# Merge gates kept raw until the merge, and the convolution's SiLU as one ScalarE function, in a one-layer hybrid decoder

## Chip, cores and metric

The kernel runs on one core of one Trainium2 chip. The metric is the device time of one execution in microseconds (us). All arithmetic is in float32; the large matrix products are made of three passes of a rounded float32 type (fp32r).

## What is computed

One layer takes 256 prompt tokens and 64 sample tokens (8 sequences of 8), so 320 columns in all, through a SwiGLU feed-forward, a token mixer and a second SwiGLU feed-forward. The change touches three places of the mixer: the SiLU behind the short convolution, and the two sigmoid gates of the merge. The reference, cut to them:

```
qk_pre, mv, mo, mif, aq, ak, av, gm, ga = split_cols(h @ w_in)
qk, conv_new = causal_conv(qk_pre, conv_buf, conv_w, conv_b)
qk = jax.nn.silu(qk).astype(f32)
mq = qk[..., :QK_WIDTH // 2].reshape(B, T, M_HEADS, M_DK)
mk = qk[..., QK_WIDTH // 2:].reshape(B, T, M_HEADS, M_DK) * (M_DK ** -0.5)
...
merged = jax.nn.sigmoid(gm) * (hm.astype(dt) @ w_pm) + jax.nn.sigmoid(ga) * (ha.reshape(B, T, A_WIDTH).astype(dt) @ w_pa)
return merged @ w_out, (k_new, v_new, C1, n1, m1, conv_new)
```

`hm` is the mLSTM's output, `ha` that of the dilated attention. M_DK is 256, so the factor on `mk` is 1/16.

## The kernel before

The program is a list of jobs that `run_job` (L272) walks in a fixed order. A job is a matrix product of 256 output rows: its weights come in chunks of 128x1024 values (512 KB, tile `raw`, five buffers). Each chunk is split by ScalarE into a rounded half `hi` (L225) and by VectorE into the remainder `lo` (L226), three buffers each, and TensorE then makes 24 matmuls of 320 columns from it into the PSUM tile `fg` (two buffers). A split is written into the program two chunks ahead of its matmuls. When a job's last chunk is done, its result is taken out of PSUM by an "evac" function during the next job.

Between the chunks, generators are stepped: the evac functions that yield (list `every`), the mLSTM recurrence (`mlstm`, L994, in `odd`, so every second chunk), the prompt attention (`even`) and the sample attention (`slow`, 8 steps in 15 chunks). What a generator issues at a step goes into the same in-order queue of its engine as the splits. So the order of all engines is set by these steps, and an instruction that waits holds up everything behind it on its engine. All DMAs but a few are issued from the SP queue (L141), also in order.

The mixer's jobs are: attention q, k, v (4 times, `aq_evac`, `ak_evac`, `av_evac`) and the input/forget gates; then four times mLSTM v, two convolved q/k jobs (`qk_evac`, L922) and the output gate (`mo_evac`, L988); then 16 merge-gate jobs; then 8 jobs with `w_pm` (`pm_evac`, L1377), 8 with `w_pa` (`pa_evac`, L1403) and 8 with `w_out`. The sample attention reads the key and value caches during most of this, and the mLSTM reads and writes its state matrices.

`qk_evac` makes SiLU as y/(1+exp(-y)): an Exp on ScalarE (L951), 1+ and for j >= 4 also x16 on GpSimd (L952), two reciprocals on VectorE with a yield before each (L955), a product on GpSimd (L956), then the store to `qk_d`. `sigmoid_evac` (L978) takes a gate out of PSUM on VectorE (L409), makes an Exp on ScalarE (L981), 1+ on GpSimd (L982), two reciprocals on VectorE (L985) and a store to DRAM; the four `mo` jobs and the 16 merge-gate jobs use it. The merge jobs load a gate back (`load_pair`) and multiply.

GpSimd also makes `qm` (L1037) and `ks` (L1048), the stationary operands of the mLSTM's small matmuls, and `qbd` (L702) for the sample attention. ScalarE changes its function table where Exp, Ln, Sqrt and SiLU follow each other; these ACT_TABLE_LOAD instructions are put in when the program is built.

Of the kernel before, what the change touches and what calls it, by code (L numbers as in the profile page):

```python
# [9 lines left out]
F32 = mybir.dt.float32  # L10
F32R = mybir.dt.float32r
AF = mybir.ActivationFunctionType
OP = mybir.AluOpType
# [17 lines left out]
C_MV, C_MO, C_MIF, C_AQ, C_AK, C_AV, C_GM, C_GA = 2048, 3072, 4096, 4104, 5128, 6152, 7176, 9224  # L31
# [97 lines left out]
def decoder_kernel(tc, I, O, K):  # L129
    nc = tc.nc  # L130
    V, S, G, T = nc.vector, nc.scalar, nc.gpsimd, nc.tensor
# [8 lines left out]
    def dma(out, in_):  # L140
        nc.sync.dma_start(out, in_)  # L141
# [4 lines left out]
    def bcast(ap, n, at=1):  # L146
        shape = list(ap.shape)
        shape.insert(at, n)
        idx = [slice(None)] * len(ap.shape)
        idx.insert(at, None)  # L150
        return ap[tuple(idx)].to_broadcast(shape)
# [6 lines left out]
    def later(fn, n=1):  # L158
        later_q.append([n, fn])
# [23 lines left out]
    def spawn(g, lst=None, first=False):  # L183
        lst = every if lst is None else lst
        lst.insert(0 if first else len(lst), g)
# [44 lines left out]
    def wsrc(w, k0, nk, c0):  # L230
        return w[k0 * 128:(k0 + nk) * 128, c0:c0 + 256].rearrange("(k p) c -> p k c", p=128)
# [3 lines left out]
    def add_job(w, k0, nkt, c0, mov, evac, kind="w", setup=None):  # L235
        cs = []
        if kind == "mif":
            cs.append((len(chunks), 0, 16))
            chunks.append((w[0:D, C_MIF:C_MIF + 8].rearrange("(k p) c -> p k c", p=128), 16, "mif"))
        else:  # L240
            k = 0
            while k < nkt:
                nk = min(4, nkt - k)
                cs.append((len(chunks), k, nk))
                chunks.append((wsrc(w, k0 + k, nk, c0), nk, "w"))
                k += nk
        jobs.append((cs, nkt, mov, evac, kind, setup))
# [95 lines left out]
    gate_d = dp.tile([16, 128, 2 * NT], F32, name="gate_d")  # L343
# [26 lines left out]
    def t_tile(dt=F32, name="tt"):  # L370
        return xp.tile([128, 2, NT], dt, tag="t", bufs=19, name=name)
# [36 lines left out]
    def times_rstd(out, ps):  # L408
        V.tensor_tensor(out, ps[:, :, 0:NT], bcast(rstd, 2), op=OP.mult)  # L409
# [96 lines left out]
    w_in = I["w_in"][0]  # L506
# [11 lines left out]
    def m3_full(name):  # L518
        return mxt([128, 3, 257], "m3", 3, name)
# [402 lines left out]
    def qk_evac(ps, j):  # L922
        pret = m3_full("pre").rearrange("p a b -> p (a b)")
        pre = pret[:, 0:694].rearrange("p (m c) -> p m c", m=2)
        V.tensor_tensor(pre[:, :, 3:259], ps[:, :, 0:SEQ], bcast(rstd[:, 0:SEQ], 2), op=OP.mult)
        pres = pre[:, :, 259:347].rearrange("p m (b c) -> p m b c", b=8)
        V.tensor_tensor(pres[:, :, :, 3:11], ps[:, :, SEQ:NT].rearrange("p m (b t) -> p m b t", b=8),
                        bcast(rstd[:, SEQ:NT].rearrange("p (b t) -> p b t", b=8), 2), op=OP.mult)
        G.memset(pre[:, :, 0:3], 0.0)
        G.tensor_copy(pres[:, :, :, 0:3], convst[:, 2 * j:2 * j + 2].rearrange("p m (b c) -> p m b c", b=8))  # L930
        cvn = M["cvn"]
        G.tensor_copy(cvn[:, 2 * j:2 * j + 2, 0:3], pre[:, :, 256:259])
        G.tensor_copy(cvn[:, 2 * j:2 * j + 2, 3:27].rearrange("p m (b c) -> p m b c", b=8), pres[:, :, :, 8:11])
        yield
        y = t_tile(F32, "y")
        for m in range(2):
            if m:
                yield
            kt = 2 * j + m
            for i in range(4):  # L940
                w = gv[:, G_CW + 16 * i + kt:G_CW + 16 * i + kt + 1]
                for o, x in ((y[:, m, 0:SEQ], pre[:, m, i:i + SEQ]),
                             (y[:, m, SEQ:NT].rearrange("p (b t) -> p b t", b=8), pres[:, m, :, i:i + 8])):
                    if i == 0:
                        S.activation(o, x, AF.Identity, scale=w, bias=gv[:, G_CB + kt:G_CB + kt + 1])
                    else:
                        V.scalar_tensor_tensor(o, x, w, o, op0=OP.mult, op1=OP.add)
        yield
        yv = y
        e = pret[:, 0:2 * NT].rearrange("p (m c) -> p m c", m=2)  # L950
        S.activation(e, yv, AF.Exp, scale=-1.0)  # L951
        G.tensor_scalar(e, e, 1.0, 1.0 if j < 4 else 16.0, op0=OP.add, op1=OP.mult)  # L952
        for m in range(2):
            yield
            V.reciprocal(e[:, m], e[:, m])  # L955
        G.tensor_tensor(e, yv, e, op=OP.mult)  # L956
        yield
        dma(qk_d[j].rearrange("p (a n) -> p a n", a=2), e)
        M["qk"] += 1
        if M["qk"] == 2:  # L960
            spawn(mlstm(), odd)
        if M["qk"] == 8:
            spawn(conv_out(), even)

    def conv_out():
        yield
        for q in range(4):
            ps = bg_tile()
            for k in range(4):
                c0 = 27 * (4 * q + k)  # L970
                tr(ps[:, k * 128:(k + 1) * 128], M["cvf"][:, c0:c0 + 128])
            cs = m3_full("cs").rearrange("p a b -> p (a b)")[:, 0:512]
            S.copy(cs[0:27], ps[0:27])
            later(lambda cs=cs, q=q: dma(O["conv_prompt"].rearrange("o b r c -> (o b r) c")[:, q * 512:(q + 1) * 512], cs[0:3]), 2)
            later(lambda cs=cs, q=q: dma(O["conv_sample"].rearrange("o b r c -> (o b r) c")[:, q * 512:(q + 1) * 512], cs[3:27]), 2)
            yield

    def sigmoid_evac(ps, dst):  # L978
        t = t_tile(F32, "sg")
        times_rstd(t, ps)  # L980
        S.activation(t, t, AF.Exp, scale=-1.0)  # L981
        G.tensor_scalar(t, t, 1.0, None, op0=OP.add)  # L982
        for m in range(2):
            yield
            V.reciprocal(t[:, m], t[:, m])  # L985
        later(lambda: dma(dst, t.rearrange("p a n -> p (a n)")), 2)

    def mo_evac(ps, h):  # L988
        yield from sigmoid_evac(ps, mo_d[h])
        yield  # L990
        yield
        M["mo"] = h
# [321 lines left out]
    for h in range(4):  # L1314
        add_job(w_in, 0, 16, C_MV + h * 256, mov_x, lambda ps, h=h: mv_evac(ps, h))
        for j in (h, h + 4):
            add_job(w_in, 0, 16, j * 256, mov_x, lambda ps, j=j: qk_evac(ps, j))
        add_job(w_in, 0, 16, C_MO + h * 256, mov_x, lambda ps, h=h: mo_evac(ps, h))
    for j in range(8):
        add_job(w_in, 0, 16, C_GM + j * 256, mov_x, lambda ps, j=j: sigmoid_evac(ps, gate_d[j]))  # L1320
    for j in range(8):
        add_job(w_in, 0, 16, C_GA + j * 256, mov_x, lambda ps, j=j: sigmoid_evac(ps, gate_d[8 + j]),
                setup=(lambda: spawn(presplit("hr"))) if j == 7 else None)


# [5 lines left out]
    def split_act(r, pool_tile):  # L1331
        hi, lo = pool_tile(F32R, "bh"), pool_tile(F32R, "bl")
        split(r, hi, lo)
        return hi, lo
# [3 lines left out]
    def presplit(key):  # L1338
        while key not in M:
            yield  # L1340
        for h in range(2):
            PRE[key, h] = split_act(M[key][h], t_tile)
            yield
# [33 lines left out]
    def pm_evac(ps, j):  # L1377
        sg = GT.pop(j)
        MT[j] = sg
        V.tensor_tensor(sg, ps[:, :, 0:NT], sg, op=OP.mult)  # L1380

    def pa_open():
# [19 lines left out]

    def pa_evac(ps, j):  # L1403
        sg = GT.pop(j)
        V.tensor_tensor(sg, ps[:, :, 0:NT], sg, op=OP.mult)
        V.tensor_tensor(sg, sg, MT[j], op=OP.add)
        H_H[j], H_L[j] = split_act(sg, h_tile)
# [8 lines left out]
    for j in range(8):  # L1416
        add_job(I["w_pm"][0], 0, 8, j * 256, mov_b, lambda ps, j=j: pm_evac(ps, j),
                setup=lambda j=j: pm_setup(j))
    for j in range(8):
        add_job(I["w_pa"][0], 0, 8, j * 256, mov_b, lambda ps, j=j: pa_evac(ps, j),  # L1420
                setup=lambda j=j: pa_setup(j))
# [48 lines left out]
    def last_tr(m):  # L1470
        xn, a = Y["xn"], bg_tile()
        for t, t0 in enumerate(TOK):
            tr(a[:, t * 128:(t + 1) * 128], xn[:, m, t0:t0 + 128])
        return a
# [204 lines left out]
    a = last_tr(1)  # L1679
# [56 lines left out]
```

## Time and profile before

| | |
|---|---|
| three timed runs | 2787.8, 2794.57, 2795.02 us (median 2794.57) |
| profiled execution, its own time | 2789.53 us |
| its span in the trace | 2787.7 us |
| busy in the span: TensorE, VectorE, ScalarE, GpSimd | 2730.3, 1633.2, 1082.7, 231.4 us |
| mean DMA rate | 200 GB/s |
| mixer with sample attention and mLSTM | about 980 to 1700 us of the span |

The span runs from the first to the last instruction. PE is TensorE's matmul row, DVE is VectorE, ACT ScalarE, POOL GpSimd and SP the queue that issues DMAs. A matmul is pipelined, so PE's busy time overstates its work; its waits and its granted clock are the better reading. "DMA share" is the mean busy share of the 16 DMA engines.

### The profile page before, as it was taken

What the parts mean: (1) busy time and instruction counts of PE and PEld (TensorE: products, weight loads), DVE (VectorE), ACT (ScalarE), POOL (GpSimd) and SP (SyncE); (2) the same over time, 40 slices, a digit from 0 to 9 for tenths busy, and PEclk for the clock granted to TensorE, in tenths of its full rate; (3) what the DMA queues carried; (4) which work ended last, traced back from release to release, by engine and by line L of the source; (5) the groups of instructions that cost most, each with busy time, mean ns of one, the idle gap of its engine ahead of it and who ended that gap; (6) DMA issues with size and microseconds to landing.
All of it is one profiled execution on the core that took longest, in us unless ns stands there. A gap on an engine that the chain in (4) does not pass through costs nothing.

```text
span 2787.7 us, 51237 instructions
## 1 busy us (share of the span) xinstructions
PE 2730.3 (98%) x21522; PEld 2678.7 (96%) x21522; DVE 1633.2 (59%) x1863; ACT 1082.7 (39%) x1364; POOL 231.4 (8%) x258
## 2 busy tenths in 40 slices
PE   9999999999999999989999999999999999999998
PEld 8999999999999999988889889999999999999998
DVE  6444444444446656977988886755444444444444
ACT  5333333333335333434443433444333333333344
POOL 0100000000000000122322210000000000000000
PEclk9999999999999999989999999999999999999999
DMA  6555555555556689999999988655554555545543
GB/s 216 160 158 182 157 166 165 156 162 161 162 156 208 206 223 294 277 289 271 305 293 315 315 267 281 210 190 159 167 165 154 168 163 160 164 153 168 165 151 114
DMA packets 507764, 557.22 MB, mean 200 GB/s; under 512 B 30157, under 2 KB 452605, under 8 KB 507509
## 3 DMA queue, kind: packets, MB, share of 16 engines
q1 hardware_dynamic: 506828, 552.43, 65.1%
q8 instruction: 168, 2.75, 0.4%
q10 hardware_dynamic: 704, 1.52, 0.2%
q14 instruction: 64, 0.52, 0.1%
HBM read 521.58 MB, written 32.28 MB: 199 GB/s over the span
## 4 chain that ended last, share of the span: by engine, by line
PE 84%; DMA 10%; DVE 3%; issue 1%; SPq 1%; ACT 1%; POOL 0%; POOLq 0%; DVEq 0%; ACTq 0%
PE fg L144 80%; PE bg L144 3%; DMA raw<-in_w_in_dram 3%; DMA kraw<-in_cache_k_dram 3%; DMA vt<-in_cache_v_dram 1%; DVE lo L226 1%; PE bg L337 1%; SPq L141 1%; DVE sg L985 1%; DMA vh<-vm_d 1%; ACT hi L225 0%; DVE kd L654 0%; DMA gate_d<-sg 0%; DMA vm_d<-stage 0%; DMA vq<-vm_d 0%
## 5 line engine op out<-in xcount | busy, mean ns | idle before, releaser
L226 DVE TENSOR_TENSOR lo<-raw,hi 128x1024 fp32r<-128x1024 f32 (+1 forms) x780 | 956.2, 1233 | 841.3 <-ACT hi L225 825.1
L144 PE MATMUL fg<-xh,lo 128*128 128x320 f32 x4240 | 1272.3, 301 | 15.2 <-DVE lo L226 15.2
L144 PE MATMUL fg<-xh,hi 128*128 128x320 f32 x4240 | 1280.4, 303 | 4.6 <-ACT hi L225 4.5
L144 PE MATMUL fg<-xl,hi 128*128 128x320 f32 x4240 | 1270.2, 301 | 0.0
L225 ACT CAST hi<-raw 128x1024 fp32r<-128x1024 f32 (+1 forms) x780 | 795.5, 1026 | 1024.0 <-PE fg L144 830.4
L144 PEld LDWEIGHTS fg<-xh,lo 128*128 128x128 f32 x4240 | 805.1, 190 | 19.2 <-DVE lo L226 18.9
L144 PEld LDWEIGHTS fg<-xh,hi 128*128 128x128 f32 x4240 | 805.2, 190 | 7.1 <-ACT hi L225 5.8
L144 PEld LDWEIGHTS fg<-xl,hi 128*128 128x128 f32 x4240 | 805.4, 190 | 0.6
L144 PE MATMUL fg<-hh,hi 128*128 128x320 f32 x1408 | 424.3, 301 | 0.0
L144 PE MATMUL fg<-hh,lo 128*128 128x320 f32 x1408 | 421.6, 299 | 0.0
L144 PE MATMUL fg<-hl,hi 128*128 128x320 f32 x1408 | 421.6, 299 | 0.0
L144 PEld LDWEIGHTS fg<-hh,hi 128*128 128x128 f32 x1408 | 266.8, 189 | 1.7 <-issue 1.6
L144 PEld LDWEIGHTS fg<-hl,hi 128*128 128x128 f32 x1408 | 266.8, 190 | 1.0 <-issue 1.0
L144 PEld LDWEIGHTS fg<-hh,lo 128*128 128x128 f32 x1408 | 266.8, 189 | 0.0
L464 POOL TENSOR_TENSOR gt<-gt,rstd 128x640 f32<-128x640 f32 x44 | 68.0, 1545 | 1725.7 <-ACT gt L463 1725.7
L144 PE MATMUL fg<-bh,hi 128*128 128x320 f32 x512 | 153.5, 300 | 0.0
L144 PE MATMUL fg<-bh,lo 128*128 128x320 f32 x512 | 153.3, 299 | 0.0
L144 PE MATMUL fg<-bl,hi 128*128 128x320 f32 x512 | 153.3, 299 | 0.0
L654 DVE STREAM_TRANSPOSE kd<-kraw 128x1024 f32<-128x1024 f32 x80 | 96.4, 1219 | 28.1 <-DMA kraw<-in_cache_k_dram 28.0
L144 PEld LDWEIGHTS fg<-bh,hi 128*128 128x128 f32 x512 | 97.0, 189 | 0.2 <-issue 0.2
L144 PEld LDWEIGHTS fg<-bl,hi 128*128 128x128 f32 x512 | 97.0, 189 | 0.0
L144 PEld LDWEIGHTS fg<-bh,lo 128*128 128x128 f32 x512 | 97.0, 189 | 0.0
(297 smaller groups left out, 1512.1 us busy)
## 6 DMA issues: line engine op xcount, KB each, us to landing
raw<-in_w_in_dram SPq DMA_DIRECT2D x176, 512.0 KB
raw<-in_w_ffb_in_dram SPq DMA_DIRECT2D x176, 512.0 KB
raw<-in_w_ffa_in_dram SPq DMA_DIRECT2D x175, 512.0 KB
raw<-in_w_ffa_out_dram SPq DMA_DIRECT2D x80, 512.0 KB
raw<-in_w_ffb_out_dram SPq DMA_DIRECT2D x80, 512.0 KB
kraw<-in_cache_k_dram SPq DMA_DIRECT2D x96, 256.0 KB
vt<-in_cache_v_dram SPq DMA_DIRECT2D x128, 192.0 KB
kraw<-in_cache_k_dram SPq DMA_DIRECT2D x32, 512.0 KB
```

The costliest lines, as they stand in the source:

```text
L141: nc.sync.dma_start(out, in_)
L144: T.matmul(out, a, b, start=start, stop=stop, **kw)
L225: S.copy(hi[:, :nk], t[:, :nk])
L226: V.tensor_tensor(lo[:, :nk], t[:, :nk], hi[:, :nk].bitcast(F32), op=OP.subtract)
L337: T.transpose(out, in_, ident[:k, :k])
L464: G.tensor_tensor(gt, gt, bcast(rstd, 2), op=OP.mult)
L654: V.transpose(kd[:, 2 * pr:2 * pr + 2].rearrange("p a b -> p (a b)"), t.rearrange("p a b -> p (a b)"))
L985: V.reciprocal(t[:, m], t[:, m])
```

## The change

The convolution's SiLU becomes one ScalarE function, with a scaled copy for the four k jobs. The 16 merge gates are only multiplied by `rstd` and stored; their sigmoid is made by ScalarE at the merge. The output gate `mo` keeps the old way.

```
@@ qk_evac
         e = pret[:, 0:2 * NT].rearrange("p (m c) -> p m c", m=2)
-        S.activation(e, yv, AF.Exp, scale=-1.0)
-        G.tensor_scalar(e, e, 1.0, 1.0 if j < 4 else 16.0, op0=OP.add, op1=OP.mult)
-        for m in range(2):
-            yield
-            V.reciprocal(e[:, m], e[:, m])
-        G.tensor_tensor(e, yv, e, op=OP.mult)
+        S.activation(e, yv, AF.Silu)
+        if j >= 4:
+            S.activation(e, e, AF.Copy, scale=1.0 / 16.0)
+        yield
         yield
         dma(qk_d[j].rearrange("p (a n) -> p a n", a=2), e)
@@ new, beside sigmoid_evac
+    def gate_evac(ps, dst):
+        t = t_tile(F32, "sg")
+        times_rstd(t, ps)
+        later(lambda: dma(dst, t.rearrange("p a n -> p (a n)")), 1)
@@ the 16 merge-gate jobs
-        add_job(w_in, 0, 16, C_GM + j * 256, mov_x, lambda ps, j=j: sigmoid_evac(ps, gate_d[j]))
+        add_job(w_in, 0, 16, C_GM + j * 256, mov_x, lambda ps, j=j: gate_evac(ps, gate_d[j]))
...
-        add_job(w_in, 0, 16, C_GA + j * 256, mov_x, lambda ps, j=j: sigmoid_evac(ps, gate_d[8 + j]),
+        add_job(w_in, 0, 16, C_GA + j * 256, mov_x, lambda ps, j=j: gate_evac(ps, gate_d[8 + j]),
@@ pm_evac and pa_evac
         sg = GT.pop(j)
+        S.activation(sg, sg, AF.Sigmoid)
         V.tensor_tensor(sg, ps[:, :, 0:NT], sg, op=OP.mult)
```

The change also moves instructions. The convolution is done one step sooner, so the mLSTM starts, and then stays, two chunks (48 of the large matmuls) earlier in TensorE's order; the sample attention stays where it was.

ScalarE, around the output gate of head 2, where the mLSTM makes the norm of head 0 (L1195 and L1196 before, L1198 and L1199 now). Before:

```order
L225 CAST hi<-raw 128x1024
L951 ACTIVATE pre<-y 128x640
L981 ACTIVATE sg<-sg 128x640
L225 CAST hi<-raw 128x1024
L1186 ACTIVATE re<-hh 128x640
L1099 ACTIVATE kw<-bg,aeT 128x256 x2
L225 CAST hi<-raw 128x1024 x2
L1195 ACT_TABLE_LOAD
L1195 ACTIVATE re<-bg,epst 128x320
L1196 ACT_TABLE_LOAD
```

Now:

```order
L225 CAST hi<-raw 128x1024
L951 ACT_TABLE_LOAD
L951 ACTIVATE pre<-y 128x640
L953 ACTIVATE pre<-pre 128x640
L979 ACT_TABLE_LOAD
L979 ACTIVATE sg<-sg 128x640
L225 CAST hi<-raw 128x1024
L1198 ACT_TABLE_LOAD
L1198 ACTIVATE re<-bg,epst 128x320
L1199 ACT_TABLE_LOAD
```

Two table loads and the scaled copy now stand ahead of the split of the next chunk. Over the whole program there are 29 table loads where there were 18: ten of the new ones stand in the convolution and output-gate jobs, one at the first merge job.

VectorE, in the merge-gate jobs late in the sample attention (`sm` and `kd` are its tiles, `hh` the mLSTM's). Before:

```order
L654 STREAM_TRANSPOSE kd<-kraw 128x1024
L409 TENSOR_TENSOR sg<-fg,rstd 128x640
L226 TENSOR_TENSOR lo<-raw,hi 128x1024 x2
L654 STREAM_TRANSPOSE kd<-kraw 128x1024
L985 RECIPROCAL sg<-sg 128x320
L226 TENSOR_TENSOR lo<-raw,hi 128x1024
L1201 TENSOR_TENSOR hh<-hh,re 128x640
L1203 SCALAR_TENSOR_TENSOR hh<-hh,gv,sgm 128x320 x2
L985 RECIPROCAL sg<-sg 128x320
L226 TENSOR_TENSOR lo<-raw,hi 128x1024
L409 TENSOR_TENSOR sg<-fg,rstd 128x640
```

Now:

```order
L654 STREAM_TRANSPOSE kd<-kraw 128x1024
L409 TENSOR_TENSOR sg<-fg,rstd 128x640
L226 TENSOR_TENSOR lo<-raw,hi 128x1024
L1204 TENSOR_TENSOR hh<-hh,re 128x640
L1206 SCALAR_TENSOR_TENSOR hh<-hh,gv,sgm 128x320 x2
L226 TENSOR_TENSOR lo<-raw,hi 128x1024
L654 STREAM_TRANSPOSE kd<-kraw 128x1024
L226 TENSOR_TENSOR lo<-raw,hi 128x1024 x2
L409 TENSOR_TENSOR sg<-fg,rstd 128x640
```

The reciprocals ahead of the remainders `lo` are gone, and the mLSTM's `hh` comes earlier.

GpSimd, the mLSTM's head 2 from its norm on. Before:

```order
L1187 TENSOR_TENSOR re<-re 128x320
L982 TENSOR_SCALAR sg<-sg 128x640
L1037 TENSOR_TENSOR qm<-qsc,mixc 128x64 x2
L1048 TENSOR_TENSOR ks<-kf,ks 64x256 x2
L982 TENSOR_SCALAR sg<-sg 128x640
L1048 TENSOR_TENSOR ks<-kf,ks 64x256
L1037 TENSOR_TENSOR qm<-qsc,mixc 128x64 x2
```

Now:

```order
L1190 TENSOR_TENSOR re<-re 128x320
L1040 TENSOR_TENSOR qm<-qsc,mixc 128x64 x2
L1051 TENSOR_TENSOR ks<-kf,ks 64x256 x3
L1040 TENSOR_TENSOR qm<-qsc,mixc 128x64 x2
```

No gate instruction stands ahead of `qm` and `ks` any more.

## Rows read from the trace of the kernel before

**Rows 1.** The page, busy time, share and instructions of each engine over the span.

```profile
PE 2730.3 (98%) x21522; PEld 2678.7 (96%) x21522; DVE 1633.2 (59%) x1863; ACT 1082.7 (39%) x1364; POOL 231.4 (8%) x258
```

**Rows 2.** Stretches: us, busy of PE, PEld, DVE, ACT, POOL; PEclk, DMA share, GB/s.

```profile
980.00:1330.00 350.00, 330.50 (x3092) 312.60 (x3091) 257.47 (x412) 136.93 (x232) 57.17 (x83) 0.97 0.94 271
1120.00:1680.00 560.00, 526.14 (x5015) 489.35 (x5008) 469.88 (x647) 234.87 (x378) 139.17 (x182) 0.98 0.98 291
1330.00:1470.00 140.00, 130.72 (x1231) 119.91 (x1230) 122.44 (x172) 62.33 (x103) 40.35 (x53) 0.98 1.01 300
1470.00:1610.00 140.00, 132.87 (x1273) 123.03 (x1272) 116.86 (x144) 57.16 (x91) 36.77 (x44) 1.00 1.03 314
1610.00:1700.00 90.00, 87.47 (x833) 83.08 (x835) 73.15 (x83) 38.10 (x55) 13.74 (x9) 1.00 0.91 276
1429.00:1436.00 7.00, 6.45 (x23) 6.05 (x24) 6.75 (x7) 4.31 (x8) 0.86 (x1) 0.51 1.03 280
```

**Rows 3.** Waits of PE, 1330 to 1700 us: total us, times, longest.

```profile
PE fg L144 <- DVE lo L226: 5.4, 7, 1.4
PE bg L144 <- POOL qm L1037: 3.3, 4, 1.3
PE bg L144 <- POOL ks L1048: 2.5, 3, 1.2
PE bg L337 <- ACT re L1195: 1.9, 1, 1.9
PE bg L337 <- ACT pts L768: 1.8, 1, 1.8
```

**Rows 4.** VectorE in order of time at 1573 us: start, us, instruction.

```profile
1573.66 2.11 DVE L985 RECIPROCAL sg<-sg 128x320 f32<-128x320 f32 x1
1575.69 1.16 DVE L226 TENSOR_TENSOR lo<-raw,hi 128x1024 fp32r<-128x1024 f32 x1
```

**Rows 5.** Groups by line: busy us, mean ns, idle before and releasers.

```profile
L985 DVE RECIPROCAL sg<-sg 128x320 f32<-128x320 f32 x40 | 85.0, 2126 | 0.0
...
L955 DVE RECIPROCAL pre<-pre 128x320 f32<-128x320 f32 x16 | 34.1, 2132 | 0.0
...
L982 POOL TENSOR_SCALAR sg<-sg 128x640 f32<-128x640 f32 x20 | 36.2, 1812 | 178.5 <-ACT sg L981 148.8 <-issue 11.1 <-DMA kraw<-in_cache_k_dram 9.8
...
L956 POOL TENSOR_TENSOR pre<-y,pre 128x640 f32<-128x640 f32 x8 | 12.6, 1577 | 57.0 <-DVE pre L955 57.0
...
L952 POOL TENSOR_SCALAR pre<-pre 128x640 f32<-128x640 f32 x8 | 6.1, 765 | 62.0 <-ACT pre L951 58.3 <-DMA vq<-vm_d 3.7
...
L981 ACT ACTIVATE sg<-sg 128x640 f32<-128x640 f32 x20 | 14.7, 737 | 88.9 <-DVE sg L409 79.7 <-issue 8.1 <-DMA raw<-in_w_in_dram 1.1
```

**Rows 6.** ScalarE in order of time at a table load, head 0's norm.

```profile
1325.72 1.28 ACT L1195 ACT_TABLE_LOAD   x1
1327.02 0.53 ACT L1195 ACTIVATE re<-bg,epst 128x320 f32<-128x320 f32 x1
```

**Rows 7.** Waits of ScalarE, 1120 to 1470 us.

```profile
ACT hi L225 <- PE fg L144: 47.3, 23, 5.4
```

**Rows 8.** Waits of ScalarE, 1330 to 1700 us.

```profile
ACT sg L981 <- DVE sg L409: 74.6, 15, 9.3
...
ACT hi L225 <- DMA raw<-in_w_in_dram: 13.5, 5, 4.1
```

**Rows 9.** Waits of PE, 1610 to 1700 us.

```profile
PE fg L144 <- DVE lo L226: 2.0, 3, 0.7
PE fg L144 <- ACT hi L225: 0.5, 1, 0.5
```

**Rows 10.** Waits of PE, 980 to 1330 us.

```profile
PE fg L144 <- DVE lo L226: 8.4, 4, 6.6
...
PE bg L144 <- POOL qm L1037: 3.4, 1, 3.4
PE fg L144 <- ACT hi L225: 3.2, 1, 3.2
```

More of the change, by code (lines that the diff above doesn't have):

```diff
@@ L1404, in pa_evac @@
         sg = GT.pop(j)
+        S.activation(sg, sg, AF.Sigmoid)
         V.tensor_tensor(sg, ps[:, :, 0:NT], sg, op=OP.mult)
```

## Prediction

> **What bounds the kernel now.** I begin with the page's busy times [rows 1]: PE 98%, VectorE 59%, ScalarE 39%, GpSimd 8%. A share over the whole span says only that TensorE sets the time nearly everywhere; what this change touches lies in one stage, so the stretches come next [rows 2]. From 1120 to 1680 us VectorE is busy 469.88 of 560 us, 84%, and the DMA share is 0.98. So in this stage three things are nearly full at once: TensorE, VectorE and the DMA engines. Third come PE's own waits, since only they lengthen the program. From 1330 to 1700 us five groups hold 5.4 + 3.3 + 2.5 + 1.9 + 1.8 = 14.9 us [rows 3]: PE waits for the remainder `lo`, for `qm` and `ks` from GpSimd, and for a PSUM buffer that ScalarE has not yet emptied (the `ident` transposes). A stall has a second price. From 1429 to 1436 us the granted clock is 0.51 [rows 2], the lower of TensorE's two levels (1.2 of 2.4 GHz), right behind one of the waits on ScalarE; those 7 us at half speed lose 7 x 0.49 = 3.4 us. What the stretch could give back is 14.9 + 3.4 = 18.3 us.
>
> Are those waits due to what the change removes? Three rows say yes. At 1573.66 a reciprocal of 2.11 us stands right ahead of a `lo` on VectorE [rows 4]. GpSimd's sum for a gate takes 1.812 us [rows 5] and stands ahead of `qm` and `ks` in its queue, where the order shows nothing of the gates afterwards. And ScalarE, in order, sat waiting for the gate's PSUM copy on VectorE for 74.6 us in 15 waits [rows 8], with the next splits queued behind that Exp.
>
> **The change, part by part.**
>
> VectorE loses the 16 reciprocals of the convolution and the 32 of the merge gates (40 less the 8 that `mo` keeps): 34.1 + 32 x 2.126 = 102.1 us [rows 5], all of it in the full stage. Its load from 1120 to 1680 falls from 469.88 to about 368 us, 66%.
>
> GpSimd loses 16 x 1.812 = 29.0, 12.6 and 6.1, together 47.7 us [rows 5]. It is not full, but it stands ahead of small operands that PE waits for.
>
> ScalarE keeps the convolution's 8 functions and moves 16 gate functions of 0.737 us from the gate jobs to the merge jobs. What it gains is four scaled copies, at the 0.737 us of the same shape [rows 5], and 11 table loads. A load is 1.28 us and the next ACTIVATE starts 1.30 us after the load does [rows 6], so 11 x 1.30 + 4 x 0.737 = 17.2 us, 15.9 of them in the convolution stage. The cover there is that a split is early: 23 times the cast waited for PE to free its buffer, 2.06 us on average [rows 7]. In five places one load of 1.30 us goes in ahead of a cast and fits. At three of the four output gates a load and a copy go in, 2.04 us, which just fits; at the fourth two loads and a copy, 3.34 us, which sticks out by 1.3. If all cover were gone it would be 17.2 us, and the least is 1.3, since the mean wait hides short ones. I take 3 us, near the lower end, because VectorE, the other half of the split, is relieved in the same place.
>
> The merge itself: one function of 0.737 us before each product, ahead of a chunk's cast; a pm or pa job has two chunks, and PE is never short of operands after 1700 us, so I cost it at nothing. If a gate's load came late there, ScalarE's casts would now queue behind that wait, where before only VectorE's product did.
>
> DMA: the same bytes. Gate stores leave about three chunks sooner, the q/k stores no longer make the SP queue wait for GpSimd's product, and the mLSTM's loads move two chunks forward. No cost, no gain that a row shows.
>
> How much of the 18.3 us can come back depends on the DMA queues. From 1470 to 1610 the DMA share is 1.03 at 314 GB/s [rows 2], the highest in these rows. If 1.03 is the ceiling, 1330 to 1470 can shrink by 140 x (1 - 1.01/1.03) = 2.7 us, 1470 to 1610 not at all, and 1610 to 1700, with a share of 0.91, can lose its PE waits of 2.0 + 0.5 = 2.5 us [rows 9]: 5.2 us. If it is no ceiling, 18.3 us. Against a hard ceiling stands that casts waited only 13.5 us for raw weights in this stretch and 74.6 us sat in front of gates [rows 8]; for it, that every stretch here is at 1.0. I take the middle, 11.75 us. The Trainium skill, "DMA: Bandwidth & Descriptors", Specifications, gives a limit of about 358 GB/s from HBM for a core. By that the 314 GB/s would be no ceiling and the sum would be 18.3 - 3 = 15.3 us faster; no row here goes over 314, so I do not use it.
>
> The sum: -11.75 + 3 = -8.75 us. Against the profiled execution's own 2789.53 us that is 2780.8. The four executions shown (three timed, one profiled) average 2791.7, 2.2 us above the profiled one, so I put the forecast at **2783 us**; the median shown, 2794.57, is 5.0 us above the profiled execution. That is 0.4% under the median. About 0.3%, or 8.4 us, is what a measurement can tell from no change: the boundaries are 2786.2 and 2803.
>
> **The rivals.**
>
> (a) The DMA holds. If the ceiling is real, the stalls on VectorE and GpSimd were time in which the DMA caught up, and PE will wait for raw weights in their place. Gain 5.2, cost 3: 2.2 us, so 2791.7 - 2.2 = 2789.5 us. For it: shares of 1.01 and 1.03; against: the small waits for raw weights. Its sign would be casts waiting much longer than 13.5 us for `raw`. Chance 0.30.
>
> (b) ScalarE's table switches become the late half of the split, and the kernel is slower. The place is the convolution jobs, 1120 to 1470 us, where ten loads and four copies land between casts. It decides if the added 1.30 to 3.34 us per place exceed what a cast is early by. Where PE is held by DMA the mean of 2.06 us [rows 7] may hide casts that were not early at all. Price: the full 17.2 us against a gain held to 5.2: 12 us slower, 2803.7 us. For it: PE did wait 3.2 us for `hi` in 980 to 1330 [rows 10]. Chance 0.08.
>
> A variant of it: a switch costs ScalarE twice what the load's row shows, because the engine must first drain. Then 11 x 2.6 + 2.9 = 31.5 us land on the engine and, held to the same 5.2 us gain, the time is 2818 us. Against it, in the order of time the ACTIVATE behind a load starts 1.30 us after it [rows 6], and nothing else is lost. Chance 0.02. The Trainium skill, "ScalarE: Activation LUTs", What ACT_TABLE_LOAD costs, has this rule: about 1.28 us for the load and 1.38 us for a drain, 2.66 us for every switch, and it advises not to alternate sets. The trace agrees with the 1.28 us and shows no drain.
>
> (c) A larger gain: the stretch before the gates is freed too. From 980 to 1330 us PE waited 8.4 + 3.4 + 3.2 = 15.0 us for `lo`, `qm` and `hi` [rows 10], and the clock of 0.97 over 350 us [rows 2] lost another 10.5. With the convolution's reciprocals and products gone and the mLSTM's loads two chunks away, about half of 25.5 could go as well: 2783 - 12.7 = 2770 us. Against it: those waits are long and few (6.6 us at one of them), which looks like a late transfer and not like a full engine. Chance 0.14.
>
> **How the numbers follow.** The forecast has 0.46, (a) 0.30, (b) and its variant 0.10, (c) 0.14. The forecast and (c) are faster by over 0.3%, 0.60; (a) is within, 0.30; (b) is slower, 0.10. The range reaches from 2765, somewhat under the centre of (c), to 2796, which takes in (a) and a little ScalarE cost on top; it leaves out (b) and the part of (c) in which everything goes.
>
> **What would show it.** VectorE's busy time falls by 102 us, GpSimd's by about 48, ScalarE's rises by about 17. If the argument holds, PE's waits for `qm` and `ks` after 1330 us nearly vanish and those for `lo` halve; VectorE is under 70% in the stage; the DMA share stays at 1.0 or above, at a higher rate. (a) is right if waits for `raw` take the place of the others and the rate stays near 300. (b) is right if PE waits for `hi` behind a table load in the convolution jobs. The forecast fails most simply if a new long stall, with a half-clock interval behind it, appears where the mLSTM's two chunks earlier start meets the cache loads: one of 6.6 us and its 3.4 us at the lower clock would undo it.

## The result and the profile after

The changed kernel takes 2778.19 us (median of 6 runs, 2769.49 to 2781.38) where the kernel before takes 2793.42 in the same comparison (also 6 runs): a ratio of 0.994 [0.9927, 0.9954], 15.2 us faster by the medians. That is past the 0.3% that can be told from no change. The forecast was 2783 us, in the range of 2765 to 2796. The profiled execution after took 2780.48 us (span 2778.7), 9.0 less than the profiled one before, so the two profiles show only some 9 of the 15 us. Keep that in mind for every row below.

The page, busy time of each engine, against [rows 1]:

```profile
PE 2727.4 (98%) x21522; PEld 2678.3 (96%) x21522; DVE 1534.0 (55%) x1815; ACT 1104.3 (40%) x1379; POOL 179.5 (6%) x226
```

VectorE does 1633.2 - 1534.0 = 99.2 us less, GpSimd 51.9 less, ScalarE 21.6 more. The groups by line show what is left of the lines of [rows 5] (busy us, mean ns, idle before and releasers):

```profile
L983 DVE RECIPROCAL sg<-sg 128x320 f32<-128x320 f32 x8 | 17.0, 2127 | 0.0
...
L951 ACT ACT_TABLE_LOAD x5 | 6.4, 1283 | 10.8 <-DVE y L947 8.6 <-issue 2.2
L1383 ACT ACTIVATE sg<-sg 128x640 f32<-128x640 f32 x8 | 5.9, 739 | 2.0 <-DMA sg<-gate_d 2.0
L951 ACT ACTIVATE pre<-y 128x640 f32<-128x640 f32 x8 | 5.9, 738 | 5.1 <-issue 2.7 <-DVE y L947 2.3
L1409 ACT ACTIVATE sg<-sg 128x640 f32<-128x640 f32 x8 | 5.9, 737 | 6.7 <-DMA sg<-gate_d 6.7
```

Eight reciprocals are left, those of `mo`. The SiLU and the sigmoid cost what the Exp did, 0.74 us each. At the merge ScalarE did wait for a gate's load, 2.0 + 6.7 us in all. PE has no wait from 1700 to 2000 us, so that cost nothing.

The stretches, columns as in [rows 2]:

```profile
980.00:1330.00 350.00, 332.47 (x3133) 314.46 (x3133) 237.87 (x417) 154.72 (x253) 45.40 (x76) 0.98 0.97 276
1120.00:1680.00 560.00, 529.51 (x5016) 495.72 (x5009) 382.11 (x606) 247.66 (x381) 89.98 (x148) 0.97 0.99 297
1330.00:1470.00 140.00, 131.34 (x1230) 121.45 (x1229) 101.28 (x160) 62.81 (x99) 25.79 (x45) 0.96 1.02 310
1470.00:1610.00 140.00, 134.03 (x1280) 125.26 (x1279) 88.92 (x126) 54.36 (x83) 22.42 (x34) 0.98 1.03 311
1610.00:1700.00 90.00, 90.00 (x934) 86.67 (x933) 51.42 (x69) 37.07 (x49) 2.48 (x2) 1.00 0.91 284
...
1531.00:1537.00 6.00, 5.61 (x21) 4.91 (x22) 1.03 (x7) 3.36 (x7) 0.37 (x1) 0.61 1.08 303
```

VectorE is at 382.11 of 560 us, 68%, where it was at 84%. The DMA did not get easier: its share is as high as before in each stretch from 1330 us on, and from 1330 to 1470 the rate rose from 300 to 310 GB/s. PE's waits, 1330 to 1700 us, against [rows 3]:

```profile
PE bg L144 <- DMA vh<-vm_d: 6.0, 1, 6.0
PE bg L144 <- ACT cs L971: 3.2, 1, 3.2
PE fg L144 <- DVE lo L226: 2.8, 2, 2.1
PE fg L144 <- ACT hi L225: 1.2, 1, 1.2
PE bg L144 <- ACT re L1198: 1.0, 1, 1.0
PE bg L144 <- POOL qm L1040: 0.5, 1, 0.5
```

The waits for `qm` and `ks` fell from 5.8 to 0.5 us, those for `lo` from 5.4 to 2.8, and the two `ident` transposes wait no more. In their place stand a load that lands late (`vh`, the mLSTM's values of the last head) and a copy, `cs`. ScalarE's own waits in the same stretch, against [rows 8], say what `cs` was late for:

```profile
ACT hi L225 <- PE fg L144: 113.5, 59, 6.2
...
ACT hi L225 <- DMA raw<-in_w_in_dram: 16.4, 4, 8.8
...
ACT cs L971 <- DMA out_conv_sample_dram<-cs: 8.3, 1, 8.3
```

The 74.6 us in which ScalarE sat in front of a gate are gone, and casts wait for PE instead, which is what one wants: the split is early. Before, that first group was

```profile
ACT hi L225 <- PE fg L144: 31.0, 17, 3.9
```

But `cs` waited 8.3 us for a store that had to free its buffer. Both new waits of PE have a DMA behind them. Around the end of the `vh` wait, from 1531 to 1537 us, the granted clock is 0.61: partly at the lower level (1.2 GHz). Nor did the clock recover in this stretch as a whole. By the rows of 140 us, the lower clock lost an estimated 140 x 0.02 = 2.8 us before, and 140 x 0.04 + 140 x 0.02 = 8.4 us after.

From 980 to 1330 us, against [rows 10], the waits that matter are now:

```profile
PE fg L144 <- DVE lo L226: 6.7, 2, 5.5
PE bg L144 <- DVE lo L226: 6.4, 1, 6.4
```

The waits for `qm` (3.4) and `hi` (3.2) of [rows 10] are gone; those for `lo` rose from 8.4 to 13.1 us. Both long ones have a transfer near them. Ahead of the 5.5 us, VectorE waits 7.91 us for `kraw`, the key cache. The 6.4 us end at a matmul that reads `vh`, loaded from 1306.87 us on, so the name `lo` in that row may not be the true cause.

**Where the time was won.** In the changed kernel the mLSTM's matmuls stand elsewhere in PE's order, so the progress of the two programs cannot be compared in the middle of the stage. It can in a run described below, the changed kernel with one more step ahead of the q/k store: there PE's matmuls stand in exactly the order of the kernel before. These are the starts of the same matmuls of the large products (tile `fg`), in us, in one profiled execution of each:

| before | one step later | gained since 980 us |
|---|---|---|
| 980.05 | 980.45 | 0 |
| 1194.27 | 1191.94 | 2.7 |
| 1201.15 | 1194.58 | 7.0 |
| 1215.08 | 1206.51 | 9.0 |
| 1330.02 | 1327.14 | 3.3 |
| 1345.10 | 1338.07 | 7.4 |
| 1702.66 | 1691.70 | 11.4 |

9.0 us are there by 1215 us, in a stretch for which the forecast had booked no gain. Part of them is lost and won again up to 1345 us; another 4.0 us come after that.

The largest step, some 4 us at 1201 us, can be followed back. In the order of time, the kernel before:

```profile
1164.62 1.58 POOL L956 TENSOR_TENSOR pre<-y,pre 128x640 f32<-128x640 f32 x1 [5.64 <-DVE pre L955]
1166.23 0.34 SPq L141 DMA_DIRECT2D qk_d<-pre  x1
1188.03 3.11 SPq L141 DMA_DIRECT2D kraw<-in_cache_k_dram  x3
1197.67 1.25 DVE L654 STREAM_TRANSPOSE kd<-kraw 128x1024 f32<-128x1024 f32 x1 [12.58 <-DMA kraw<-in_cache_k_dram]
1201.15 0.64 PE L144 MATMUL fg<-xh,lo 128*128 128x320 f32 x1 [6.58 <-DVE lo L226]
```

With the SiLU as one function (the run with one step later):

```profile
1156.81 0.55 SPq L141 DMA_DIRECT2D qk_d<-pre  x1
1181.74 1.86 SPq L141 DMA_DIRECT2D kraw<-in_cache_k_dram  x3
1191.10 1.25 DVE L654 STREAM_TRANSPOSE kd<-kraw 128x1024 f32<-128x1024 f32 x1 [8.86 <-DMA kraw<-in_cache_k_dram]
1194.58 0.40 PE L144 MATMUL fg<-xh,lo 128*128 128x320 f32 x1 [2.35 <-DVE lo L226]
```

Before, the q/k store in SP's in-order queue goes out only when GpSimd's product has ended, and that product waits for VectorE's reciprocals. Everything behind the store is late with it: the load of `kraw` is issued 6.3 us later, VectorE stands in front of it for 12.58 us, `lo` is late, and PE waits 6.58 us. At the same matmul PE waits 6.95 us in the run with the gates alone, 0.46 in the one with the SiLU alone and 1.15 in the changed kernel, so it is the SiLU's part that removes this wait. How much of the 6.3 us is the store itself is not separated from the weights ahead of it in the queue, whose buffers come free when `lo` is made (from 1150 to 1182 us SP waits 11.2 us for `lo` before and 6.9 there). VectorE was not full here; what its reciprocals made late was the queue.

### The profile page after: what moved, and what is told of

Read it like the earlier page. It is cut to its first block, busy times and chain, and to the rows that moved or that the text cites. A ratio compares the mean times of both kernels' runs of the same rounds, so it can differ in the third digit from the quotient of the medians.

```text
span 2778.7 us, 51128 instructions
## 1 busy us (share of the span) xinstructions
PE 2727.4 (98%) x21522; PEld 2678.3 (96%) x21522; DVE 1534.0 (55%) x1815; ACT 1104.3 (40%) x1379; POOL 179.5 (6%) x226
## 2 busy tenths in 40 slices
DMA packets 507763, 557.22 MB, mean 201 GB/s; under 512 B 30156, under 2 KB 452604, under 8 KB 507508
## 4 chain that ended last, share of the span: by engine, by line
PE 86%; DMA 9%; DVE 3%; ACT 1%; issue 1%; POOLq 0%; POOL 0%; SPq 0%; ACTq 0%; DVEq 0%
PE fg L144 82%; DMA raw<-in_w_in_dram 4%; PE bg L144 3%; DMA kraw<-in_cache_k_dram 2%; PE bg L337 1%; DVE lo L226 1%; DMA vt<-in_cache_v_dram 1%; ACT hi L225 0%; DVE kd L654 0%; DMA out_C_sample_dram<-C 0%; DMA vh<-vm_d 0%; DMA out_conv_sample_dram<-cs 0%; DVE y L947 0%; DMA vq<-vm_d 0%; DMA mo_d<-sg 0%
```

## The experiments

Each run is compared with the kernel before on the same chip; the ratio has its 95% interval. In us, a ratio's distance from another is multiplied by 2793. The changed kernel was not timed again beside these runs, so its distance from one of them is best read from the ratios; by their intervals it is open by some 6 us either way.

**The parts alone.** First the SiLU without the gates, which then take the old `sigmoid_evac` again:

```
-... lambda ps, j=j: gate_evac(ps, gate_d[j]))
+... lambda ps, j=j: sigmoid_evac(ps, gate_d[j]))
-        S.activation(sg, sg, AF.Sigmoid)
```

> The convolution's SiLU as one function alone; the merge gates go the old way (28 table loads). Removed from VectorE: 16 reciprocals, 34 us; from GpSimd 18.7 us; added to ScalarE: 15.9 us. My reading (the gain sits in the gate jobs, where ScalarE and VectorE wait in turn): 0 to 5 us faster than before. If table loads were the price to fear: 3 to 12 us slower than before. If any relief of VectorE counted in proportion: a third of the 15 us, 5 us faster.

Measured: 2786.66 against 2793.54 us, 0.9976 [0.9967, 0.9986], 6.9 us faster. That is more than the 0 to 5 expected of it: the prediction had booked this part as a cost of ScalarE.

Then the gates without the SiLU:

```
-        S.activation(e, yv, AF.Silu)
...
+        S.activation(e, yv, AF.Exp, scale=-1.0)
+        G.tensor_scalar(e, e, 1.0, 1.0 if j < 4 else 16.0, op0=OP.add, op1=OP.mult)
+        for m in range(2):
+            yield
+            V.reciprocal(e[:, m], e[:, m])
+        G.tensor_tensor(e, yv, e, op=OP.mult)
```

> Raw merge gates alone; the convolution goes the old way (19 table loads). Removed from VectorE: 32 reciprocals, 68 us; from GpSimd 29 us; one table load added. My reading: 9 to 14 us faster than before, most of the whole change. If the convolution's table loads cost what ScalarE spends on them, this one is faster than the whole change by 3 us or more. If the DMA engines hold the stage, this and the other part do not add up to 15 us: each alone gets less than 6.

Measured: 2785.07 us, 0.9963 [0.9949, 0.9976], 8.5 us faster by the medians. That is a little under the 9 to 14 expected. Its one profiled execution, 2789.69 us, shows none of the gain, so only the wait at 1201 us above is read from it. 6.9 + 8.5 = 15.4 us, the whole: within some 6 us the parts add up. By what was expected, each alone would have got less than 6 us if the DMA held the stage; it did not come out so, though the runs below show that the DMA takes a part.

**The price of table loads.** Two tiny functions ahead of each SiLU force two more switches:

```
+        S.activation(epst2, epst, AF.Silu)
+        S.activation(epst2, epst, AF.Exp)
         S.activation(e, yv, AF.Silu)
```

> The changed kernel with 16 more table loads: ahead of each convolution SiLU two functions on one column switch the table away and back. ScalarE gets 16 x 1.30 us and 16 x about 0.2 us more, 24 us. My reading (a split is early, the loads run under waits): 0 to 5 us slower than the changed kernel. If a load delays the splits by its full length: about 24 us slower. If a switch costs twice its row: 42 us or more.

Measured: 2779.06 us, 0.9945 [0.9928, 0.9962], against 0.994 of the change: 0.9 us above it by the medians and 1.4 by the ratios, far inside the intervals. The loads are there; ScalarE's busy time on the page and the groups of the first two functions' lines show them:

```profile
PE 2726.2 (98%) x21522; PEld 2677.3 (96%) x21522; DVE 1532.8 (55%) x1815; ACT 1127.2 (41%) x1411; POOL 181.3 (7%) x226
...
L952 ACT ACT_TABLE_LOAD x8 | 10.3, 1283 | 0.1
L953 ACT ACT_TABLE_LOAD x8 | 10.3, 1283 | 3.6 <-DVE y L947 3.2 <-issue 0.3
```

16 more loads and 16 small functions are 1127.2 - 1104.3 = 22.9 us of ScalarE, more than the whole change adds, and no time that can be told from zero; 22.9 us would have shown. Rival (b) falls.

**What the gates' 8.5 us are.** Three kernels each put one thing back into the new gate function: ScalarE's place in the lockstep, GpSimd's pass, VectorE's reciprocals (here into a scratch tile, so that the result stays).

```
@@ one pass on ScalarE
         times_rstd(t, ps)
+        S.activation(t, t, AF.Copy)
@@ one pass on GpSimd
         times_rstd(t, ps)
+        G.tensor_scalar(t, t, 1.0, None, op0=OP.mult)
@@ two reciprocals on VectorE
         times_rstd(t, ps)
+        u = t_tile(F32, "su")
+        for m in range(2):
+            yield
+            V.reciprocal(u[:, m], t[:, m])
```

> The changed kernel with one copy by ScalarE over each raw gate before its store (0.74 us x16, no table load): ScalarE again waits for VectorE's PSUM copy in front of the next split, while reciprocals and GpSimd's sum stay away. If that lockstep made the gate stage's stalls: most of the gates' 8 to 10 us is lost again, so 6 to 10 us slower than the changed kernel. If VectorE's reciprocals or GpSimd's sums were the cause: 0 to 2 us slower.

> The changed kernel with one product by 1 on GpSimd over each raw gate before its store (about 1.8 us x16), straight from VectorE's PSUM copy. GpSimd then stands ahead of the small operands qm and ks again. If that order made PE wait: 2 to 5 us slower than the changed kernel (the waits for qm and ks were 5.8 us before). If only VectorE's load or the lockstep mattered: 0 to 1 us.

> The changed kernel with the 32 reciprocals put back on VectorE at the old steps of the gate jobs, into a scratch tile (68 us of VectorE), without ScalarE's and GpSimd's part; the store follows later, as before. If VectorE's load is the cause: 6 to 10 us slower than the changed kernel. If the order of ScalarE or GpSimd was: 0 to 3 us slower.

Measured: 2778.99 us, 0.9948 [0.9931, 0.9965]; 2781.33 us, 0.9956 [0.994, 0.9972]; 2780.41 us, 0.9959 [0.9944, 0.9973]. Each did put back what it was meant to. ScalarE's waits, 1330 to 1700 us, with its pass:

```profile
ACT sg L989 <- DVE sg L409: 57.6, 16, 7.4
```

GpSimd's group with its pass:

```profile
L989 POOL TENSOR_SCALAR sg<-sg 128x640 f32<-128x640 f32 x16 | 38.7, 2417 | 157.9 <-DVE sg L409 101.4 <-DMA out_C_sample_dram<-C 19.5 <-ACT hi L225 16.7
```

VectorE's 32 reciprocals took 68.2 us.

57.6 us of ScalarE waiting in front of a gate is most of the 74.6 of [rows 8], and it cost 2.2 us by the ratios and 0.8 by the medians. The two intervals, 0.0017 and 0.0013 to either side, leave such a difference open by some 0.002, or 6 us, so this is nothing that can be told from zero. The lockstep that looked so large in a view of waits was mostly idle time of an engine that had time. The passes on GpSimd and VectorE cost 4.5 and 5.3 us by the ratios, 3.1 and 2.2 by the medians, neither clear of zero. The three together would make 12.0 by the ratios and 6.1 by the medians, about the 8.5 that the gates bring. None of them alone shows the whole 8.5, but with 6 us open either way GpSimd's or VectorE's part could still be most of it. Which of the three the gates' gain comes from, or whether it needs two at once, stays open.

**Is it the shift?** The convolution ends one step sooner, which moves the mLSTM two chunks. One more yield moves it back:

```
         yield
         yield
+        yield
         dma(qk_d[j].rearrange("p (a n) -> p a n", a=2), e)
```

> The changed kernel with one more step before the q/k store, so that the mLSTM stands where it stood before (two chunks later in TensorE's order); nothing else differs. If part of the convolution's 7 us came from that shift: slower by up to 7 us than the changed kernel. If it came from VectorE, GpSimd and the SP queue: the same within 3 us.

Measured: 2779.14 us, 0.9952 [0.9935, 0.9968], 1 us above the changed kernel by the medians and 3.4 by the ratios. The gain is there without the shift. That the shift brings or costs a few us is not excluded: 3.4 lies within the 6 us that are open.

**How much does the DMA hold back?** Both kernels with only the first unit's value-cache load kept, and its tiles used for the other fifteen. That takes 39.6 of 557.2 MB away, all in this stage, and leaves VectorE, ScalarE and PE their work.

```
-                if u < 16:
+                if u == 0:
                     later(lambda pc=pc: load_v(u, pc), 1 + n)
+                elif u < 16:
+                    VT[u, pc] = VT[0, pc]
```

> The kernel before, with the value cache of the sample attention loaded for its first unit alone and used for all 16 (15 of 16 loads left out, about 39 MB of some 190 MB in the stage; the sample attention's result is then that of wrong values). It shows what the DMA engines cost the kernel before. If they hold the stage: 25 us or more faster than before. If VectorE and the queues hold it: under 10 us faster.

> The changed kernel with the same loads left out. If a DMA ceiling took a part of the change's gain, this stands further below the run before it than 15 us: 20 us or more between the two. If no ceiling took part: 15 us within 3. If the gain was only DMA order (fewer collisions): less than 10 us between the two.

Measured on one chip: the kernel before so relieved 2767.91 us, 0.9912 [0.9899, 0.9926]; the changed one 2737.53 us, 0.9803 [0.9788, 0.9818]. The relief gives the old kernel 2792.22 - 2767.91 = 24.3 us, just under the 25 expected if the DMA held it, and the new one (0.994 - 0.9803) x 2793 = 38 us. The change is worth 2767.91 - 2737.53 = 30.4 us when the DMA has room, twice the 15.2 it is worth as it stands and clear of the noise. The rows say why. The relieved kernel before, its full stage, and PE's waits from 980 to 1700 us:

```profile
1120.00:1680.00 560.00, 539.16 (x5171) 505.47 (x5170) 484.77 (x659) 245.40 (x388) 140.44 (x180) 0.99 0.80 240
...
PE fg L144 <- DVE lo L226: 8.1, 9, 2.7
PE bg L144 <- POOL qm L1039: 5.6, 4, 3.4
PE bg L337 <- ACT re L1197: 3.3, 2, 3.1
```

The relieved changed kernel, the same two views:

```profile
1120.00:1680.00 560.00, 554.96 (x5373) 526.22 (x5373) 400.61 (x619) 266.65 (x400) 90.59 (x147) 1.00 0.83 253
...
PE bg L144 <- POOL ks L1053: 2.4, 2, 2.1
PE fg L144 <- DVE lo L226: 2.1, 1, 2.1
PE bg L144 <- POOL qm L1042: 0.5, 1, 0.5
```

With the DMA share at 0.80, the old kernel still waits for `lo`, `qm` and `re`, on VectorE, GpSimd and ScalarE, with VectorE at 484.77 of 560 us, 87%. The changed one waits 5.0 us in 720, in the three groups shown, and the clock over them is 1.00. So the waits named in the prediction were real and the change removes most of them; in the kernel as it stands these loads take half of that back. The edit also takes them out of SP's queue, so the pair does not say whether it is the DMA engines or the queue that holds. "The DMA" stands below for the two together.

**Can the DMA's part be had by ordering?** Two attempts on the changed kernel. The 32 small loads that gather `q4` from DRAM go to GpSimd's queue, so that SP is free for weights; and, on top of it, the last head's values are loaded sooner.

```
@@ fill(i) of q4
-                    dma(q4[32 * i:32 * i + 32, :, j], ...)
+                    G.dma_start(q4[32 * i:32 * i + 32, :, j], ...)
@@ second kernel, besides
                     load_head(h + 1)
+                    if h == 2:
+                        load_vals(3)
```

> The changed kernel with the 32 small loads of q4 (32 KB each) issued from GpSimd's queue and not from SP's. In the trace of the changed kernel SP spends about 1 us on each of 16 of them at 1294 to 1304 us, the DMA share falls under 0.4 there, and PE waits 6.4 us right behind. If issue on SP is what starves the DMA engines there: 5 to 12 us faster than the changed kernel, with the clock's half-speed interval gone. If the DMA engines only used the pause to catch up: the same within 3 us. If GpSimd takes longer to issue and holds qbd, qm and ks: slower by 3 to 8 us.

> As the run before, and the mLSTM's values of the last head (vh, on which PE waited 6.0 us in the changed kernel) loaded some five chunks earlier, into the same three buffers. If each of these two waits was on the path: 8 to 18 us faster than the changed kernel. If the DMA engines hold the stage, the wait moves to other loads: 0 to 4 us.

Measured: 2778.95 us, 0.9954 [0.994, 0.9967], and 2779.75 us, 0.9959 [0.9944, 0.9975]: no gain. In the changed kernel 16 of the `q4` loads go out between 1290 and 1304 us, and from 1290 to 1310 the DMA moves 193 GB/s at a share of 0.73 (0.55 from 1294 to 1304 and 0.31 from 1296 to 1300). With `q4` on GpSimd's queue the same 20 us have 279 GB/s, but the next 20 fall to 193 where they had 311. Over 1270 to 1330 us the changed kernel has

```profile
1270.00:1330.00 60.00, 47.30 (x404) 43.23 (x404) 36.27 (x68) 29.81 (x44) 10.88 (x20) 0.89 0.89 256
```

and the one with `q4` on GpSimd's queue

```profile
1270.00:1330.00 60.00, 42.75 (x363) 38.83 (x363) 34.03 (x61) 28.73 (x43) 19.85 (x36) 0.83 0.83 245
```

so the hole in the DMA was moved and not filled. PE's waits changed their names. With both edits, 980 to 1700 us (in a profiled execution of 2787.66 us, the slowest of the six):

```profile
PE fg L144 <- DVE lo L226: 11.0, 4, 5.4
PE bg L144 <- POOL re L1190: 7.8, 1, 7.8
PE bg L144 <- DMA vt<-in_cache_v_dram: 6.0, 7, 3.3
PE bg L144 <- ACT cs L971: 4.1, 1, 4.1
```

The wait for `vh` is gone and its time stands elsewhere, in part behind GpSimd: PE waits 7.8 us for its `re`, where the changed kernel waits 0.8, and GpSimd issues 16 `q4` loads, 0.55 us each, ahead of it. So the edit puts a new load on an engine that PE waits for, and the pair does not settle whether SP's queue or the DMA engines hold the stage. Whether some other order of the loads, or another queue, would shorten it was not tried.

**Table loads with the DMA relieved.** If the DMA covered the 16 extra loads, they should show once it is relieved: the edit of the table-load run on the relieved changed kernel.

> The changed kernel with the value cache loaded for the first unit alone (as in the run that leaves out 15 of 16 loads) and the 16 more table loads of the earlier run, 24 us of ScalarE. There the DMA engines gave room in which loads could hide; here they hold no longer. If table loads are covered because splits are early: 0 to 3 us slower than the same kernel without them (2737.5 us). If they were only hidden under waits for DMA: 6 to 24 us slower.

Measured: 2745.18 us, 0.9826 [0.9812, 0.9839], against 0.9803: 0.0023, or 6.4 us, for some 23 us of ScalarE. By the intervals that is open by some 5.6 us, so it is only just clear of zero. About a quarter now shows. PE's waits from 980 to 1700 us rose from 5.0 to 8.7 us, and all that are left stand behind GpSimd's small operands:

```profile
PE bg L144 <- POOL ks L1055: 6.4, 2, 3.9
PE bg L144 <- POOL qm L1044: 2.3, 2, 1.7
```

So part of what covers ScalarE's extra work seems to be the DMA ceiling itself. The two relieved kernels ran on two chips, each beside the kernel before, so it is the ratios that are compared.

## Why the prediction was right, and where its sum was off

**What bounds the kernel.** Right. TensorE, VectorE and the DMA were nearly full together; VectorE's share fell from 84% to 68% and the DMA's stayed.

**Busy times.** Forecast -102, -48 and +17 us for VectorE, GpSimd and ScalarE; measured -99.2, -51.9 and +21.6. VectorE's load from 1120 to 1680 us came to 382 us and not 368, since more of the program passes in the same stretch.

**The gain.** This is the mis-sized term: "I take the middle, 11.75 us", between 5.2 and 18.3, all of it from 1330 us on. There the same matmuls gain about 4 us in the run whose order allows the comparison, close to the end held by the DMA, 5.2. The 3.4 us of clock in the 18.3 did not come back: in the changed kernel the lower clock cost more than before. And of the three rows that were to tie the waits to the change, ScalarE's 74.6 us could be put back at no price that can be measured. But 7.4 us came from 980 to 1345 us, which the sum left out and gave to rival (c) alone. The reading that the longest wait there "looks like a late transfer and not like a full engine" was right: VectorE stood 12.58 us in front of `kraw`. The step that failed is another term, "No cost, no gain that a row shows", for the order of the DMAs. It names the q/k store that no longer holds the SP queue for GpSimd's product and puts it at nothing; the runs show the transfer issued 6.3 us sooner and PE's wait fall from 6.58 to between 0.46 and 2.35 us with it. The SiLU alone, whose main work lies there, gave 6.9 us. Nor was 18.3 the upper end: without the ceiling the change gives 30.4 us.

**The agreement of the profiled times** (2780.8 forecast on the profiled base, 2780.48 measured) is therefore luck: one stretch gave less, the other more. Against the measured 15.2 us, the sum of 8.75 was too small by 6.5.

**ScalarE's 3 us.** Too much as the kernel stands, as far as the noise tells: 16 further loads cost 0.9 us. Rival (b) is refuted by that run and by the result, and its sign is absent: PE's wait for `hi` after 1330 us is 1.2 us and before it there is none. The variant, a drain behind every load, has no row either. In order of time, ScalarE at a SiLU:

```profile
1283.69 1.28 ACT L951 ACT_TABLE_LOAD   x1 [6.41 <-DVE y L947]
1284.99 0.74 ACT L951 ACTIVATE pre<-y 128x640 f32<-128x640 f32 x1
```

The function starts 1.30 us after its load, as in [rows 6]. The Trainium skill, "ScalarE: Activation LUTs", What ACT_TABLE_LOAD costs, puts a switch at 2.66 us with its drain; by that the 16 extra loads would hold ScalarE for an estimated 42.6 us. The trace does not agree: the page shows 22.9 us with their functions, and ScalarE is idle for only 0.1 + 3.6 us ahead of those loads, 3.2 of it waiting for data.

**Rival (a), the DMA holds.** Half right, and the more useful half of the prediction. The ceiling is real and takes half the gain. Of its two signs one came: from 1330 to 1700 us the rate stayed near 300 GB/s (300 before, 304 after). The other was put too narrowly: waits for `raw` rose only from 13.5 to 16.4 us, and the time came back in `vh` and in `cs` behind a store.

**Rival (c), the earlier stretch is freed too.** It happened, at about 7 of the 12.7 us that it was given, and the largest step of it went by way of the SP queue.

**What would undo it.** The long stall with a half-clock interval beside it did appear, 6.0 us at `vh` and 1531 to 1537 us at 0.61, and before 1330 us two more, of 5.5 and 6.4 us. The gain held all the same. The forecast had said that one such stall would undo it; it weighed that stall against a gain of 8.75 that was too small, and the kernel before had long stalls too.

**Merge and shift.** The merge cost nothing, as booked. For the shift no cost can be told from zero.

## What to carry over

When several engines are nearly full in one stage, work taken from one of them is paid out only up to the next ceiling; to size it, run both kernels once with the suspected ceiling lowered, here by loading less. Long waits in front of an engine that has time (74.6 us here) need not be a price: put the wait back and see. Look for the gain in every stretch where the removed work stood, not only in the one where the engine is fullest. And where a wait comes from a late transfer, ask what held the queue that issued it: a store that waits for a slow engine delays every load behind it in that queue.

## What was not expected of the hardware

A table load does not always use the time in which its function waits for data. Here one stood behind the same wait of 6.41 us (the two rows of ScalarE above), and only then took its 1.28 us. Another, at 959.28 us in the kernel before, ran first, and its function then waited 1.25 us. What decides it was not tried.

The 16 DMA engines were at a share of 1.03 with 311 GB/s after and 314 before, over 140 us; 452,604 of the 507,763 packets are under 2 KB on the page. In shorter stretches the rate went higher (323 GB/s at a share of 1.02 from 1330 to 1350 us after), so a share of 1.0 is no fixed rate. The Trainium skill, "DMA: Bandwidth & Descriptors", Specifications, gives about 358 GB/s from HBM for a core; no stretch of 140 us read here came within 40 GB/s of it.

On GpSimd a product with 1.0 over 128x640 values, in place, took 2417 ns, where the gate's sum of the same shape takes 1812 ns [rows 5]. Which of place, neighbours or operation does it was not tried.
